# Matmul with batch normalisation: eight normalising instructions of VectorE rewritten to read their shift from PSUM

## The chip, the cores and the metric

The kernel runs on one core of a Trainium2 chip. A core has a matrix engine (TensorE, PE), a vector engine (VectorE, DVE), a scalar engine (ScalarE, ACT), a general engine (GpSimd, POOL), and a sync engine (SP) that here only issues DMAs. Operands lie in SBUF, results of TensorE in PSUM[...], and GpSimd is given no work on PSUM here. Each engine works its own queue in order, and engines wait for one another through semaphores. The metric is the device time of one execution in microseconds, shown as the median of several runs.

## The reference

The kernel computes a product and normalises each of its 768 columns over all 8192 rows:

```python
y = np.matmul(x, weight)                      # x (16, 512, 1024), weight (1024, 768)
mean = np.mean(y, axis=(0, 1), keepdims=True)
var = np.var(y, axis=(0, 1), keepdims=True)
y_norm = (y - mean) / np.sqrt(var + eps)
return (gamma * y_norm + beta).astype(np.float32)
```

No output value can be written before the statistics of its column are complete. For each column the kernel forms a scale and a shift, and an output is `y * scale + shift`.

## The kernel before

**Tiles.** The 768 columns are six tiles of 128 (`NT = 6`). The 8192 rows are 16 chunks of 512 (`CH = 512`, `C = 16`). The first three tiles (`GA = 3`) are treated as a group; the text calls tile `nt = 3` the fourth, `nt = 4` the fifth and `nt = 5` the sixth. A block is one tile of one chunk, 128 columns on the partitions by 512 rows, in bf16.

**First part.** While x arrives, TensorE computes the first three tiles for all chunks, and the others for the first five chunks (`EARLY = 5`). In twelve of the chunks the product of the three tiles lies with rows on the partitions (`mm_rows`), in four (`COLS`) with columns on the partitions (`mm`).

**Second part.** With the first three tiles complete, `affine_rows` forms their scale and shift, and `spread_rows` spreads both over all partitions by a product with ones: the scales into a PSUM tile `a_ps` of 128x384 (`aff[0]`), which stays there, the shifts into another, which ScalarE copies into SBUF (`sum1`). Then three streams of work run side by side:

- TensorE computes the remaining chunks of the fourth, the fifth and the sixth tile (`mm`, L196). Behind each block VectorE takes its statistics (`bn`, L316) and ScalarE copies it from PSUM to SBUF as bf16 (`keep`, L343).
- The twelve chunks with rows on the partitions are finished without TensorE: VectorE multiplies two row groups by the scales in PSUM (`norm_rows`, L283, 24 times, called a row product below), GpSimd adds the shifts from SBUF (`shift_rows`, L289, 24 times, called an add), SP stores.
- A tile with columns on the partitions and known statistics is finished in place: a block is normalised by ScalarE or VectorE (`norm`, L377 and L382), TensorE turns it back by transposes that stand between its other matmuls (`turn_y`, L398), ScalarE copies the turned block pair from PSUM into a piece of the SBUF ring (`out_copy`, L411), and SP stores it (L416).

**Scale and shift of the fourth and fifth tile.** `finish_var` has VectorE aggregate the statistics (L350), ScalarE take the square root (L351) and VectorE the reciprocal (L352). `finish_affine` then has ScalarE compute three columns of 128x1: `nscale` (L356), `scale` (L357) and `shift` (L358).

**Which engine normalises.** `outputs` goes through a tile in pairs of blocks, `b = 0` to `7`. While the row products run (the pair's due time `tb` lies below `tr + 2.0`, where `tr` is the due time of their end), the even block goes to ScalarE and the odd one to VectorE; later both go to VectorE. For the fourth tile this is so for `b = 0` to `6`, for the fifth only for `b = 0`.

**Order.** Every step is put into a list with a due time that is written by hand (`at`), the list is sorted, and the steps are issued in that order. `seq` ties each instruction to the one before it on its engine, so that the written order is the order of every queue. Semaphore waits between engines follow from the tiles that instructions read and write. PSUM tiles come from one pool of 8 buffers, one for each bank.

Of the kernel before, what the change touches and what calls it, by code (L numbers as in the profile page):

```python
# [10 lines left out]
def kernel(  # L11
# [23 lines left out]
    nc = tc.nc  # L35
# [3 lines left out]
    ALU = mybir.AluOpType  # L39
# [5 lines left out]
    P = 128  # L45
    NT = N // P
    KQ = K // 4
    CH = 512
# [9 lines left out]
    GA = 3  # L58
    COLS = (0, 5, 10, 15)
    NA = GA * P  # L60
# [16 lines left out]
    def seq(bi):  # L77

        ins = bi.ins
        prev = last.get(ins.engine)  # L80
        if prev is not None:
            tc.add_manual_dep(
                ins, prev,
                mybir.DependencyInfo(mybir.DependencyClass.NoSync, mybir.DependencyReason.DATA),
                reason="order",
            )
        last[ins.engine] = ins.name
        return bi
# [6 lines left out]
    scale = singles.tile([P, NT], f32)  # L95
    shift = singles.tile([P, NT], f32)
# [30 lines left out]
    xs, xT, py, ygrp, yrow, ops, ost, aff = {}, {}, {}, {}, {}, {}, {}, {}  # L127
# [140 lines left out]
    def spread_rows(i):  # L268

        a_ps = psum.tile([P, CH], f32, tag="b")  # L270
        aff[i] = a_ps[:, 0:NA]
        seq(nc.tensor.matmul(aff[i], full, aff["diag"][:, i], start=True, stop=True))  # L272
        if i == 1:
            seq(nc.scalar.copy(sum1, aff[i]))  # L274
# [24 lines left out]
    def y(nt, c):  # L299
        key, i = ((nt, c // GY), c % GY) if nt >= GA else ((0, c), nt)  # L300
        if key not in ygrp:
            y_sb = ypool.tile([P, GY, CH], bf16, tag="y")
            ygrp[key] = y_sb
        return ygrp[key][:, i]
# [49 lines left out]
    def finish_affine(nt):  # L354
        one = slice(nt, nt + 1)
        seq(nc.scalar.activation(nscale, rstd, AF.Identity, scale=ngamma[:, one]))  # L356
        seq(nc.scalar.activation(scale[:, one], rstd, AF.Identity, scale=gamma_sb[:, one]))  # L357
        seq(nc.scalar.activation(  # L358
            shift[:, one], mv[:, nt, 0:1], AF.Identity, bias=beta_sb[:, one], scale=nscale))

    def finish(nt):
        one = slice(nt, nt + 1)
        src = stats_of(nt) if nt < NT - 1 else fin
        seq(nc.vector.bn_aggr(mv[:, nt, :], src))
        seq(nc.scalar.activation(std[:, one], mv[:, nt, 1:2], AF.Sqrt, bias=eps_sb, scale=1.0))
        seq(nc.vector.scalar_tensor_tensor(
            tmp[:, one], mv[:, nt, 0:1], -1.0, gamma_sb[:, one], op0=ALU.mult, op1=ALU.mult,
        ))
        seq(nc.vector.reciprocal(rstd, std[:, one]))
        seq(nc.vector.tensor_mul(scale[:, one], rstd, gamma_sb[:, one]))  # L370
        seq(nc.vector.scalar_tensor_tensor(
            shift[:, one], tmp[:, one], rstd, beta_sb[:, one], op0=ALU.mult, op1=ALU.add,
        ))

    def norm(nt, c, eng):
        if eng == "act":
            seq(nc.scalar.activation(  # L377
                y(nt, c), y(nt, c), AF.Identity,
                bias=shift[:, nt:nt + 1], scale=scale[:, nt:nt + 1],
            ))  # L380
        else:
            seq((nc.vector if eng == "dve" else nc.gpsimd).tensor_scalar(  # L382
                y(nt, c), y(nt, c), scale[:, nt:nt + 1], shift[:, nt:nt + 1],
                op0=ALU.mult, op1=ALU.add,
            ))
# [39 lines left out]
    def at(t, fn, *args):  # L425
        events.append((t, len(events), fn, args))
# [85 lines left out]
    at(S + 0.9, affine_rows)  # L512
    at(S + 2.4, shift_diag)
    at(S + 4.4, spread_rows, 0)
    at(S + 5.6, spread_rows, 1)
    for nt in range(GA):
        at(S + 5.0, norm, nt, 0, "dve")
    ga = tuple(range(GA))
    tr, tk = S + 4.7, S + 6.3
    for c in range(C):  # L520
        if c in COLS:
            for nt in range(GA):
                if c:
                    at(tk - 3.4 + 0.8 * nt, norm, nt, c, "act")
            for s in range(0, RT, 2):
                at(tk + 0.7 * s, turn_y, ga, c * CH + s * P, 2)
                at(tk + 0.7 * s + 1.9, out_copy, ga, c * CH + s * P, "act")
                at(tk + 0.7 * s + 2.7, store, ga, c * CH + s * P, 2)
            tk += 9.6 if c else 7.2
        else:  # L530
            for s in range(0, RT, 2):
                at(tr, norm_rows, c, s)
                at(tr + 1.1, shift_rows, c, s)
                at(tr + 3.0, store_rows, c, s)
                tr += 1.85

    def outputs(nt, t0, step):
        for b in range(C // 2):
            tb = t0 + step * b
            if nt == NT - 2 and b >= C // 2 - HELD:  # L540
                held.append(b)
                continue
            for i in range(2):
                at(tb - 2.2 + 0.5 * i, norm, nt, 2 * b + i, "act" if tb < tr + 2.0 and i == 0 else "dve")
            at(tb, turn_y, (nt,), 2 * b * CH, 2 * RT)
            at(tb + 2.2, out_copy, (nt,), 2 * b * CH, "act")
            at(tb + 2.3, store, (nt,), 2 * b * CH, 2 * RT)
# [21 lines left out]
    for nt in range(GA, NT):  # L569
        for c in range(EARLY, C):  # L570
            if (nt, c) == (NT - 1, C - 1):
                for q in range(QPC):
                    at(pe, mm_half, q)
                    pe += 0.9
                    at(pe + 0.2, bn_half, q)
                    at(pe + (0.4 if q == 0 else 1.0), keep_half, q)
                at(pe - 2.4, sum_up)
                continue
            for jws in halves:
                unit(nt, c, MM_US / 2 + (0.12 if nt == GA else 0.17), jws)  # L580
        if nt < NT - 1:
            at(pe + 0.55, finish_var, nt)
            at(pe + 1.6, finish_affine, nt)
        else:
            at(pe + 0.55, finish, nt)
        if nt == GA:
            outputs(nt, S + 37.0, 2.3)
        elif nt < NT - 1:
            outputs(nt, pe + 4.6, 1.85)
        else:  # L590
            held_outputs(nt - 1, pe)
            last_outputs(nt, pe + 3.0)
# [39 lines left out]
```

## Time and profile before

| what | value |
|---|---|
| median of 8 runs | 219.83 us (219.18 to 220.51) |
| profiled execution | 220.45 us, of which its span is 218.6 us |
| TensorE matmul busy | 199.4 us, 91% of the span |
| VectorE busy | 155.7 us, 71% |
| GpSimd busy | 134.1 us, 61% |
| ScalarE busy | 121.2 us, 55% |
| chain that ended last | PE 74%, DVE 8%, DMA 6%, POOL 3% |
| VectorE normalising (L382) | 43 instructions, 22.0 us |
| GpSimd adds (L289) | 24 instructions, 44.2 us, from 134.8 to 182.5 us |
| VectorE row products (L283) | 24 instructions, from 133.3 to 180.4 us |

The span runs from the first instruction to the last; the rest of an execution's time lies around it. Busy time of an engine is no measure of what bounds the kernel: which engine the others wait for changes from stage to stage. The page's rows in slices of the span show the stages:

```profile
PE   7996999999999999999999999999999979997900
DVE  3220968887978789998744459988899999828900
ACT  2000563644453466645666414867767689986950
POOL 7786867778685589962558403999996973000000
```

Each digit is a slice of 5.5 us, in tenths of busy time. GpSimd's adds are the stretch of nines right of the middle. In the slice that starts at 175 us TensorE falls to 7, and in the last slices only transposes, copies and stores are left.

### The profile page before, as it was taken

The page shows a single profiled execution, that of the slowest core. Times are in us where ns is not written, and L with a number is a line of the kernel's source. Part 1 is how long each engine was busy: PE and PEld are TensorE (multiplying, and loading weights), DVE is VectorE, ACT ScalarE, POOL GpSimd, SP SyncE. Part 2 cuts the span into 40 slices and gives each one's busy share as a digit, 9 for nine tenths or more (in the row PEclk, how much of TensorE's full clock was granted, in tenths as well). Part 3 has the DMA queues.
Part 4 walks back from the last instruction along what each step waited for, and adds up shares of the span by engine and source line. Part 5 has one row for each costly group of instructions (what it writes and reads, how often), then busy time and mean ns, then how long its engine had stood idle before and what let it go on. Part 6 is the DMA issues. An engine that isn't in the chain of part 4 may idle for free.

```text
span 218.6 us, 3435 instructions
## 1 busy us (share of the span) xinstructions
PE 199.4 (91%) x1162; PEld 106.3 (49%) x1178; DVE 155.7 (71%) x263; ACT 121.2 (55%) x227; POOL 134.1 (61%) x153
## 2 busy tenths in 40 slices
PE   7996999999999999999999999999999979997900
PEld 2452454545554565645566544444444435554800
DVE  3220968887978789998744459988899999828900
ACT  2000563644453466645666414867767689986950
POOL 7786867778685589962558403999996973000000
PEclk9999999999999999999999999999999999999675
DMA  4999999999999999994000000798777989999998
GB/s 59 163 185 189 171 196 196 197 196 196 196 191 194 197 196 196 196 197 67 0 4 0 0 0 0 284 341 311 288 290 294 328 276 368 327 347 299 280 346 243
DMA packets 70161, 43.75 MB, mean 200 GB/s; under 512 B 4096, under 2 KB 69632, under 8 KB 70144
## 3 DMA queue, kind: packets, MB, share of 16 engines
q0 software_dynamic: 34624, 18.36, 61.6%
q1 hardware_dynamic: 35520, 25.18, 35.6%
q8 instruction: 9, 0.15, 0.3%
q14 instruction: 8, 0.07, 0.1%
HBM read 36.71 MB, written 25.17 MB: 283 GB/s over the span
## 4 chain that ended last, share of the span: by engine, by line
PE 74%; DVE 8%; DMA 6%; POOL 3%; issue 3%; ACT 2%; ACTq 1%; POOLq 0%
PE y_ps L196 38%; PE y_ps L186 29%; PE o_ps L398 6%; DMA w_sb<-in_weight_dram 3%; DMA ring<-in_x_dram 2%; DVE stats L316 2%; DVE y_sb L382 2%; DVE ring L283 2%; POOL w_sb L149 2%; DVE o_sb L283 1%; POOL ring L162 1%; PE y_ps L330 1%; ACT o_sb L411 1%; PE a_ps L272 1%; PE tot_ps L232 1%
## 5 line engine op out<-in xcount | busy, mean ns | idle before, releaser
L196 PE MATMUL y_ps<-xT_sb,w_sb 128*128 128x512 bf16 (+1 forms) x469 | 116.1, 381 | 3.6 <-DMA w_sb<-in_weight_dram 2.4
L196 PEld LDWEIGHTS <-w_sb 128*128 128x128 bf16 x484 | 45.9, 96 | 60.7 <-issue 4.6
L343 ACT CAST y_sb<-y_ps 128x512 bf16<-128x512 f32 x59 | 34.5, 585 | 55.0 <-DVE stats L316 52.1
L186 PE MATMUL y_ps<-w_sb,xT_sb 128*128 128x384 bf16 x384 | 63.4, 326 | 0.0
L316 DVE BATCH_NORM_STATS2 stats<-y_ps 128x6 f32<-128x512 f32 x58 | 39.2, 684 | 21.2 <-PE y_ps L196 20.0
L162 POOL DMA_DIRECT2D ring<-in_x_dram x72 | 45.2, 633 | 12.2 <-DVE xT_sb L174 6.2
L186 PEld LDWEIGHTS <-xT_sb 128*128 128x128 bf16 x384 | 37.5, 98 | 25.6
L212 POOL TENSOR_TENSOR sum<-sum,sq_sb 128x384 f32<-128x384 f32 x38 | 38.0, 1000 | 19.2 <-ACT sq_sb L208 18.0
L174 DVE STREAM_TRANSPOSE xT_sb<-ring 128x1024 f32<-128x1024 f32 (+1 forms) x34 | 39.5, 1167 | 12.1 <-DMA ring<-in_x_dram 12.1
L398 PE MATMUL o_ps<-ident,y_sb 128*128 128x128 bf16 x240 | 38.6, 231 | 4.0 <-DVE y_sb L382 2.5
L289 POOL TENSOR_TENSOR ring<-ring,sum 128x768 f32<-128x768 f32 x17 | 31.1, 1851 | 13.1 <-ACT sum L274 12.1
L215 DVE TENSOR_TENSOR sum<-y_ps,sum 128x384 f32<-128x384 f32 x48 | 26.1, 544 | 15.0 <-ACT sq_sb L208 14.1
L208 ACT ACTIVATE sq_sb<-y_ps 128x384 f32<-128x384 f32 x48 | 23.4, 492 | 15.6 <-PE y_ps L186 12.3
L221 ACT CAST y_sb<-y_ps 128x384 bf16<-128x384 f32 x48 | 22.8, 475 | 6.7 <-DVE sum L215 6.5
L411 ACT CAST ring<-o_ps 128x1024 f32<-128x1024 bf16 (+1 forms) x24 | 22.6, 951 | 4.1 <-PE o_ps L398 2.5
L398 PEld LDWEIGHTS <-y_sb 128*128 128x128 bf16 x240 | 21.0, 104 | 7.5 <-DVE y_sb L382 3.3
L382 DVE TENSOR_SCALAR y_sb<-y_sb,scale,shift 128x512 bf16<-128x512 bf16 x43 | 22.0, 563 | 0.0
L283 DVE TENSOR_TENSOR ring<-y_sb,a_ps 128x768 f32<-128x768 bf16 x17 | 15.8, 936 | 0.0
L289 POOL TENSOR_TENSOR o_sb<-o_sb,sum 128x768 f32<-128x768 f32 x7 | 13.1, 1876 | 2.9 <-DVE o_sb L283 2.9
L377 ACT ACTIVATE y_sb<-y_sb,shift,scale 128x512 bf16<-128x512 bf16 x17 | 13.5, 815 | 0.0
L155 PE MATMUL idle_ps<-idle_sb 128*128 128x512 bf16 x37 | 10.5, 449 | 1.2 <-DVE idle_sb L103 1.2
L411 ACT CAST o_sb<-o_ps 128x512 f32<-128x512 bf16 x16 | 7.9, 679 | 0.3 <-PE o_ps L398 0.3
(62 smaller groups left out, 50.1 us busy)
## 6 DMA issues: line engine op xcount, KB each, us to landing
ring<-in_x_dram POOLq DMA_DIRECT2D x56, 256.0 KB, 8.5
out_dram<-ring SPq DMA_DIRECT2D x25, 384.0 KB, 3.3
out_dram<-ring SPq DMA_DIRECT2D x16, 512.0 KB, 5.3
out_dram<-o_sb SPq DMA_DIRECT2D x16, 256.0 KB, 3.7
out_dram<-o_sb SPq DMA_DIRECT2D x7, 384.0 KB, 3.8
ring<-in_x_dram POOLq DMA_DIRECT2D x16, 128.0 KB, 5.4
w_sb<-in_weight_dram POOLq DMA_DIRECT2D x8, 96.0 KB, 4.9
w_sb<-in_weight_dram POOLq DMA_DIRECT2D x4, 192.0 KB, 6.4
```

The source lines that it names most:

```text
L162: seq(nc.gpsimd.dma_start(x_bf[32 * i:32 * i + 32], src[:, :, KQ * i:KQ * (i + 1)]))
L174: seq(nc.vector.transpose(dst[:, half, :, jw0:jw1], src[:, :, jw0:jw1]))
L186: seq(nc.tensor.matmul(y_ps, xT[c][:, jw, s * P:(s + 1) * P, e], w_sb[:, jw, e, 0:NA], start=(jw == 0 and e == 0), stop=(jw == JW - 1 and ...
L196: seq(nc.tensor.matmul(y_ps, w_sb[:, jw, e, nt * P:(nt + 1) * P], xT[c][:, jw, q0 * QR:q1 * QR, e], start=(jw == 0 and e == 0 and q0 == 0) ...
L212: seq(eng.tensor_add(acc, acc, py.pop(("sq", c, s))))
L215: seq(nc.vector.tensor_add(sum1, py["row", c, s][:, 0:NA], sum1))
L289: seq(nc.gpsimd.tensor_add(o_sb, o_sb, sum1[:, None, :].to_broadcast([P, 2, NA])))
L316: seq(nc.vector.bn_stats(stats_of(nt)[:, i, :], py[nt, c]))
L343: seq(nc.scalar.copy(y(nt, c), py.pop((nt, c))))
L382: seq((nc.vector if eng == "dve" else nc.gpsimd).tensor_scalar(y(nt, c), y(nt, c), scale[:, nt:nt + 1], shift[:, nt:nt + 1], op0=ALU.mult, ...
L398: seq(nc.tensor.transpose(dst, src, ident))
L411: seq(nc.scalar.copy(o_sb, src))
```

## The change

In `finish_affine`, for the fourth and the fifth tile, ScalarE also copies the new shift, one value for each partition, into a free column of the PSUM tile `a_ps` that holds the row scales: columns 384 and on, one for each tile. In `outputs`, a VectorE block that is normalised while the row products run gets a new form, `dve1`: a `scalar_tensor_tensor` that multiplies by the scale (a per-partition scalar in SBUF, as before) and adds a tensor, the shift's PSUM column read again for each of the 512 elements. Blocks of ScalarE, and VectorE blocks after the row products, stay as they were. These are blocks 1, 3, 5, 7, 9, 11 and 13 of the fourth tile and block 1 of the fifth, eight in all.

```diff
         a_ps = psum.tile([P, CH], f32, tag="b")
         aff[i] = a_ps[:, 0:NA]
+        if i == 0:
+            aff["shift"] = a_ps[:, NA:NA + NT - GA]
         seq(nc.tensor.matmul(aff[i], full, aff["diag"][:, i], start=True, stop=True))
...
         seq(nc.scalar.activation(
             shift[:, one], mv[:, nt, 0:1], AF.Identity, bias=beta_sb[:, one], scale=nscale))
+        if nt < NT - 1:
+            seq(nc.scalar.copy(aff["shift"][:, nt - GA:nt - GA + 1], shift[:, one]))
...
+        elif eng == "dve1":
+
+            seq(nc.vector.scalar_tensor_tensor(
+                y(nt, c), y(nt, c), scale[:, nt:nt + 1],
+                aff["shift"][:, nt - GA:nt - GA + 1].to_broadcast([P, CH]), op0=ALU.mult, op1=ALU.add,
+            ))
...
-                at(tb - 2.2 + 0.5 * i, norm, nt, 2 * b + i, "act" if tb < tr + 2.0 and i == 0 else "dve")
+                at(tb - 2.2 + 0.5 * i, norm, nt, 2 * b + i, "dve" if tb > tr + 2.0 else "dve1" if i else "act")
```

## The prediction

> **What bounds the kernel now.** I read the busy table by stage first. TensorE is over 98% busy from 20 to 150 us, so a change far from it is worth nothing there. One stage differs:
>
> ```profile
> 160.00:180.00 20.00, 17.89 (x116) 8.89 (x117) 19.64 (x25) 13.92 (x24) 16.52 (x10) 1.00 0.84 289
> 180.00:200.00 20.00, 19.81 (x153) 11.63 (x155) 14.61 (x32) 17.47 (x25) 1.99 (x1) 1.00 1.12 348
> ```
>
> The columns are the stretch, its length, busy time of PE, PE loads, VectorE, ScalarE and GpSimd, granted clock, DMA share and GB/s. In 160 to 180 us TensorE loses 2.1 us, at full clock, while VectorE is busy all the time. From 180 to 200 us it loses almost nothing. The waits of TensorE in 160 to 182 us name the cause:
>
> ```profile
> PE o_ps L398 <- ACT y_sb L377: 1.2, 2, 0.9
> PE o_ps L398 <- DVE y_sb L382: 0.8, 2, 0.5
> ```
>
> Transposes wait for normalised blocks. From the order of time, each stall counted as the late start beyond the usual 0.28 us step from the instruction before: 0.45 (starts 168.77), 0.65 (171.69), 0.40 (176.38) and 1.11 (179.75), **2.6 us** in sum. The last two name ScalarE, but ScalarE sat behind VectorE: its square root at 177.30 waited 0.98 us for the aggregate L350. Why VectorE is late, in order of time:
>
> ```profile
> 161.91 1.84 POOL L289 TENSOR_TENSOR o_sb<-o_sb,sum 128x768 f32<-128x768 f32 x1
> 163.70 1.85 POOL L289 TENSOR_TENSOR ring<-ring,sum 128x768 f32<-128x768 f32 x1
> 166.73 1.83 POOL L289 TENSOR_TENSOR o_sb<-o_sb,sum 128x768 f32<-128x768 f32 x1 [1.18 <-DVE o_sb L283]
> ```
>
> ```profile
> 162.32 3.38 DVE L382 TENSOR_SCALAR y_sb<-y_sb,scale,shift 128x512 bf16<-128x512 bf16 x1
> 167.09 1.62 DVE L382 TENSOR_SCALAR y_sb<-y_sb,scale,shift 128x512 bf16<-128x512 bf16 x1
> 173.02 0.45 DVE L382 TENSOR_SCALAR y_sb<-y_sb,scale,shift 128x512 bf16<-128x512 bf16 x1
> 177.71 1.24 DVE L382 TENSOR_SCALAR y_sb<-y_sb,scale,shift 128x512 bf16<-128x512 bf16 x1
> ...
> L382 DVE TENSOR_SCALAR y_sb<-y_sb,scale,shift x16: 404/405/411, 202.0 to 206.9; 128x512 bf16<-128x512 bf16 x16
> ```
>
> The same instruction takes 0.405 us once GpSimd is done (last line, min/median/max), but up to 3.38 us beside its adds: the first one ends at 165.70, just after the second of two adds (165.55). So the form waits for GpSimd. GpSimd then starves, since its next input stands behind that instruction on VectorE (1.18 us idle).
>
> **The change, part by part.**
>
> *Removed.* Eight such instructions: blocks 1, 3, ..., 13 of the fourth tile and block 1 of the fifth. From start to next start they cost 3.30 + 1.55 + 0.60 + 0.37 + 0.38 + 1.16 + 2.18 (the last two together) = 9.54 us.
>
> *Added on VectorE.* Eight scalar_tensor_tensor of 128x512, bf16 from SBUF with fp32 from PSUM. No such row exists. Bounds: 0.405 us (the free old form) and 0.936 us (L283, bf16 with PSUM at 768 elements). Statistics at 512 and 256 elements take 0.69 and 0.43, so 256 elements cost 0.26 us, and L283 scaled to 512 is 0.68; statistics of 512 PSUM elements take 0.69, in steps of 0.61. I take **0.61 per step, 4.9 us for eight**. Does it wait for GpSimd? L283, with the same kinds of operands, stays at 929 to 953 ns in all 24 cases, nearly all beside an add: no. [...] free form against new, eight cost 8 x (0.68 - 0.405) = 2.2 us more; by the rows, which contain the wait, VectorE saves 9.54 - 4.9 = 4.6 us. I go by the rows.
>
> *Added on ScalarE.* Two copies of 128x1. Nearest row: L356, 0.29 us; bounds 0.2 and 0.4. The first stands before the cast at 153.38, which had 0.58 us idle ahead of it: free. It waits for the row product at 151.79, done at 152.7, while the shift is done at 152.8. The next row product (153.27) now waits for the copy, done near 153.2: at most 0.1.
>
> *A new wait.* In the order of the changed program, the instruction for block 11 waits for ScalarE's **second** copy, the fifth tile's, though it reads another column. [...] By column the wait would go; by bank it stays, and decides the sum. Behind it on VectorE stand the statistics of the sixth tile's first block, the last row product (hence GpSimd's last add), and two more new instructions. The copy stands on ScalarE behind a cast, an output copy, a normalising (block 10) and three small steps.
>
> *Moved.* Nothing changes its place; no DMA is added, and SP and POOL stand in the same order. The PSUM bank of the row factors now lives until the last new instruction, where the next user is due later still: nothing.
>
> **The sum.** I carry the trace on from 162.32 us, with TensorE needing each block at its old time less what it has gained.
>
> - VectorE: block 1 162.93, row product 163.79, statistics (TensorE gives them near 164.2) 164.86, block 3 165.47 (before: about 168.6). TensorE wants it at 168.3: +0.45. Two row products and one statistics later block 5 at 168.4 (before 171.55): +0.65.
> - Statistics, row product 169.97, block 7 170.6, statistics (TensorE-bound) 171.4, row product 172.3, block 9 172.9, statistics 173.5, row product 174.35, aggregate 174.95, where before it ended at 177.26. ScalarE's normalising of block 8 ends near 173.7, wanted 174.9: +0.40.
> - ScalarE, held by the aggregate: square root 175.2, cast 175.7, output copy 176.6, block 10 at 177.3, wanted 177.15: +1.11 - 0.2. The three small steps need 0.19 + 0.19 + 0.38 (177.30 to 178.06), and the copy ends near 178.4.
> - Block 11 therefore runs 178.4 to 179.0, as late as before (178.95), though VectorE was ready at 175.45: 2.9 us idle. TensorE wants it at 180.89 - 2.4 = 178.5: -0.55.
> - Statistics 179.6, row product 180.5, two new instructions 181.7. Then the first old-form one waits for GpSimd's last add (180.5 to 182.3) and ends at 182.65; the old chain stood at 182.87. ScalarE's block 12 ends at 181.75, wanted 181.45: -0.3.
>
> Together 2.61 - 0.2 - 0.55 - 0.3 = **1.55 us**. What is late next: from 183 us VectorE and ScalarE are only 0.2 to 0.3 us ahead of before, and TensorE 1.55. That is covered by slack: VectorE idles 0.90, 1.14 and 1.55 us at 189 to 194, and the bank waits on output copies have about 2 us. If that cover were gone the gain would fall to 0.3. After TensorE's end a chain of small steps leads to the first late store (203.56). DMA lies nearly idle from about 201.4 to 203.4, and earlier stores come 3 us sooner in 165 to 180, so a shift of 1.55 fits. The final 16 stores then fill the queue at 346 GB/s as before.
>
> The profiled execution took 220.45 us (span 218.6, 1.85 outside). It gives 218.9. The median is 219.83, and the 3.38 us wait through two adds may be shorter in other runs, so I take 1.4 off it: **218.4 us**.
>
> **Rivals.**
>
> 1. *The wait for the second copy takes it all.* For: it idles a full engine for 2.9 us and its end is as late as before. Against: TensorE reaches block 11 with 1.1 us of its old stall taken away already. If the copy comes 1 us later than worked out, or the cover after 183 us is gone, 0.3 to 0.6 remains: 219.4, no change by the 0.3% (0.66 us) that can be told from noise.
> 2. *The new form is slow, and the wait passes it on: slower.* Five new instructions stand ahead of the aggregate, and the copy follows it by 3.4 us. Each 0.1 us on the form moves block 11 by 0.6 (five ahead and itself), less 0.7 us that VectorE waits for TensorE. Break-even is where block 11 ends at 180.9: 179.0 + 6x - 0.7 = 180.9, x = 0.43, a step of 1.04 us. At 1.2 us a step: 1.2 lost, about 221. Against: it would cost more than L283 with half as many elements again.
> 3. *The wait costs little, and the whole stall goes:* 2.4 us, 217.4, if ScalarE reaches its copy a microsecond earlier.
> 4. *The change doesn't do what it says:* the new form waits for GpSimd as the old. Then eight of up to 3 us remain: 219.9 or a little more. L283's even durations speak against it.
>
> **Numbers.** Forecast 0.58 (its own range 217.8 to 219.1); rival 1 0.20; rival 2 0.08; rival 3 0.09; rival 4 0.05. Faster by over 0.3%: the forecast, rival 3 and a little of rival 1, 0.68. Within: most of rival 1 and half of rival 4, 0.20. Slower: rival 2 and the rest, 0.12. Range 217.3 to 219.9: rival 3 at the low end, rival 1 at the high end, rival 2 left out.
>
> **What would show it.** L382's new line: eight at 0.65 to 0.72 us, none over 1. GpSimd's adds ending near 179 to 181, not 182.5. An idle of 2 to 3 us on VectorE before block 11, released by the new ScalarE copy. TensorE 1.3 to 1.8 us less stalled in 160 to 182, with a stall named after VectorE near 178.5. The forecast is wrong if new instructions exceed 1 us, if TensorE stalls after 183 us, or if DMA still works off old stores when the late ones start.

## The result and the profile after

| what | before | after |
|---|---|---|
| median | 220.08 us (218.58 to 222.19, 32 runs) | 217.56 us (216.66 to 218.60, 11 runs) |
| ratio after / before | | 0.9894 (0.9871 to 0.9916) |
| profiled execution (its span) | 220.45 (218.6) us | 217.78 (216.0) us |
| TensorE / VectorE busy | 199.4 / 155.7 us | 199.6 / 151.9 us |

The kernel is faster by about 2.3 us. The two profiled executions differ by 2.67 us, but part of that is not the change's: the first row product, before which both programs issue the same work, starts at 133.26 us before and at 132.27 us after. That 0.99 us is chance. All of it is there when the first matmul of `mm_rows` starts (25.75 us before, 24.76 after), and in each of the ten profiled runs below the first row product follows that matmul by 107.5 us. The page names one source of it, TensorE's first waits for the weights, 2.4 us before and 1.3 after. What follows is therefore measured from the first row product. The **stretch** from there to the first statistics of 256 rows (the last matmuls of the sixth tile) took 66.28 us before and 64.54 after, **1.74 us less**; to the end of the span it is 85.34 and 83.73, **1.61 us less**.

The busy table of the kernel after, in the same two stages and columns (stretch, its length, busy time of PE, PE loads, VectorE, ScalarE, GpSimd, granted clock, DMA share, GB/s):

```profile
160.00:180.00 20.00, 19.55 (x134) 10.13 (x135) 16.79 (x25) 16.56 (x28) 15.97 (x10) 1.00 0.99 342
180.00:200.00 20.00, 18.04 (x145) 10.81 (x146) 14.85 (x39) 16.26 (x24) 1.16 (x1) 1.00 1.01 309
```

From 160 to 180 us TensorE is now busy for 19.55 us instead of 17.89, while VectorE fell from 19.64 to 16.79. The second row isn't a new loss: the last stage, in which TensorE waits for normalised blocks in both kernels, now begins at 196.8 us and so lies inside it.

The waits of TensorE, and then those of VectorE, from 155 to 185 us (waited us, times, longest):

```profile
PE o_ps L408 <- DVE y_sb L387: 0.3, 1, 0.3
```

```profile
DVE y_sb L387 <- ACT a_ps L363: 2.8, 1, 2.8
```

Four named waits of 2.0 us have become one of 0.3. In their place VectorE waits once, for 2.8 us, for L363, ScalarE's new copy. The new instruction itself (min/median/max ns, first and last start):

```profile
L387 DVE SCALAR_TENSOR_TENSOR y_sb<-y_sb,scale,a_ps x8: 727/740/746, 161.3 to 179.7; 128x512 bf16<-128x512 bf16 x8
```

All eight take the same time, though GpSimd adds beside nearly all of them: the form doesn't wait for GpSimd. The old one took 0.41 to 3.38 us in this place. What became of the chain to block 11 is seen in the order of time, on ScalarE and then on VectorE (start, length, idle before in brackets):

```profile
173.70 0.29 ACT L353 ACTIVATE std<-mv,eps_sb 128x1 f32<-128x1 f32 x1 [0.92 <-DVE mv L352]
173.90 0.56 ACT L345 CAST y_sb<-y_ps 128x512 bf16<-128x512 f32 x1
174.36 1.01 ACT L421 CAST ring<-o_ps 128x1024 f32<-128x1024 bf16 x1
175.27 0.82 ACT L381 ACTIVATE y_sb<-y_sb,shift,scale 128x512 bf16<-128x512 bf16 x1
...
176.35 0.38 ACT L360 ACTIVATE shift<-mv,beta_sb,nscale 128x1 f32<-128x1 f32 x1
176.76 0.16 ACT L363 COPY a_ps<-shift 128x1 f32<-128x1 f32 x1
```

```profile
174.03 0.16 DVE L354 RECIPROCAL rstd<-std 128x1 f32<-128x1 f32 x1 [0.36 <-ACT std L353]
176.96 0.75 DVE L387 SCALAR_TENSOR_TENSOR y_sb<-y_sb,scale,a_ps 128x512 bf16<-128x512 bf16 x1 [2.77 <-ACT a_ps L363]
```

VectorE is ready at 174.19 us and needs only the fourth tile's shift, which has been in PSUM since 152 us. It waits for the fifth tile's copy, which stands on ScalarE behind a cast, an output copy, block 10 and three small steps. TensorE gets block 11 at 177.76 us, 0.47 us after it could have used it.

### The profile page after: what moved, and what is told of

Read it like the earlier page. It is cut to its first block, busy times and chain, and to the rows that moved or that the text cites. A ratio compares the mean times of both kernels' runs of the same rounds, so it can differ in the third digit from the quotient of the medians.

```text
span 216.0 us, 3439 instructions
## 1 busy us (share of the span) xinstructions
PE 199.6 (92%) x1162; PEld 106.5 (49%) x1178; DVE 151.9 (70%) x263; ACT 120.7 (56%) x229; POOL 133.8 (62%) x153
## 4 chain that ended last, share of the span: by engine, by line
PE 78%; ACT 5%; DMA 5%; DVE 3%; POOL 3%; issue 2%; ACTq 1%; POOLq 0%
PE y_ps L196 43%; PE y_ps L186 29%; PE o_ps L408 4%; ACT o_sb L421 3%; DMA w_sb<-in_weight_dram 3%; DMA ring<-in_x_dram 2%; POOL w_sb L149 2%; POOL ring L162 1%; ACT ring L421 1%; PE y_ps L332 1%; ACT y_sb L381 1%; DVE stats L318 1%; DVE y_sb L387 1%; PE a_ps L274 1%; PE tot_ps L232 1%
## 5 line engine op out<-in xcount | busy, mean ns | idle before, releaser
L345 ACT CAST y_sb<-y_ps 128x512 bf16<-128x512 f32 x59 | 35.1, 596 | 51.6 <-DVE stats L318 48.7
L392 DVE TENSOR_SCALAR y_sb<-y_sb,scale,shift 128x512 bf16<-128x512 bf16 x35 | 12.5, 415 | 0.0
L155 PE MATMUL idle_ps<-idle_sb 128*128 128x512 bf16 x37 | 11.0, 465 | 1.2 <-DVE idle_sb L103 1.2
```

What stands on the lines that cost most here:

```text
L345: seq(nc.scalar.copy(y(nt, c), py.pop((nt, c))))
```

## The experiments

**Theory A** is the account of the prediction: the gain is the old form's wait for GpSimd, and the wait for the second copy gives a part of it back. In each run it stands against a rival for that one step, which the expectation states. All kernels are edits of the kernel after. Runs 1 to 4 shared one set of runs of the kernel before (219.39 us, 13 runs), runs 5 to 8 another (219.64 us, 55 runs). Where nothing waits, TensorE's transposes follow one another by 0.28 us (0.06 us to the matmul between them and 0.23 us from it); a late start is what a transpose comes later than that. The last column sums the late starts from 160 us to the end of GpSimd's adds; a start that looks late only because matmul records are missing before it is left out.

| kernel | median us (runs) | ratio to before | stretch us | late starts us |
|---|---|---|---|---|
| before | | | 66.28 | 2.61 |
| after | 217.56 (11) | 0.9894 (0.9871 to 0.9916) | 64.54 | 0.73 |
| 1 after, again | 217.68 (9) | 0.9916 (0.9888 to 0.9945) | 64.53 | 0.73 |
| 2 own bank | 217.12 (6) | 0.9895 (0.9861 to 0.9929) | 63.74 | none |
| 3 fourth tile only | 216.85 (6) | 0.9877 (0.9840 to 0.9913) | 63.66 | none |
| 4 shift from SBUF | 221.68 (6) | 1.0107 (1.0071 to 1.0143) | 68.27 | 4.49 |
| 5 copies only | 219.71 (20) | 0.9999 (0.9979 to 1.0020) | 66.35 | 2.60 |
| 6 first two only | 219.62 (20) | 1.0002 (0.9978 to 1.0027) | 65.64 | 1.99 |
| 7 copy earlier | 218.32 (20) | 0.9947 (0.9923 to 0.9970) | 64.89 | 1.27 |
| 8 form doubled | 224.26 (4) | 1.0228 (1.0165 to 1.0290) | 71.35 | 4.89 |

From the statistics of 256 rows to the end of the span all ten profiled runs took 19.05 to 19.21 us: what the stretch gains arrives at the end. And up to run 7 the stretch is 63.6 to 63.8 us plus the late starts: they account for all of it.

### 1. The same kernel again

No edit.

> The changed kernel once more, to be compared with the others of this call. Both theories: 217.0 to 218.2 us. Theory A (the gain arises from 160 to 182 us alone, 1.6 to 1.7 us; the other 0.9 us of difference between the two profiles lie in the first 150 us, where the programs are the same, and are chance): the first row product starts anywhere from 132.0 to 133.6 us in this profile, and the stretch from it to TensorE's last product block is again 63.6 us within 0.3. Rival B (something in the first part became faster by 1 us): the first row product starts near 132.3 us again.

The profiled execution took 219.95 us, 2.17 more than the first, and its first row product started at 134.46 us, 2.19 later, which is outside the expected 132.0 to 133.6. In this run the page's row of the granted clock has an 8 in the two slices from 16.4 to 27.3 us, where the pages of all the others have a 9; how much of the 2.19 us that is was not tried. The stretch was 64.53, against 64.54. (Measured to the statistics of the last block of 512 rows, one block earlier, it is 63.65 and 63.66, near the 63.6 of the expectation.) So two executions of one program differ by over 2 us in the first part, and by 0.01 in the stretch: only the stretch, or the times of many runs, may be compared.

### 2. The second copy in its own bank

The fifth tile's shift goes to a free column of the other spread tile, which lies in another bank.

```diff
-        if i == 0:
-            aff["shift"] = a_ps[:, NA:NA + NT - GA]
+        aff["shift", i] = a_ps[:, NA:NA + 1]
...
-            seq(nc.scalar.copy(aff["shift"][:, nt - GA:nt - GA + 1], shift[:, one]))
+            seq(nc.scalar.copy(aff["shift", nt - GA], shift[:, one]))
...
-                aff["shift"][:, nt - GA:nt - GA + 1].to_broadcast([P, CH]), op0=ALU.mult, op1=ALU.add,
+                aff["shift", nt - GA].to_broadcast([P, CH]), op0=ALU.mult, op1=ALU.add,
```

> The fifth tile's shift goes into the other spread tile, that of the shifts, so into another PSUM bank; the rest is as changed. Theory A (block 11 waits for the second copy only because both columns share a bank): the 2.8 us idle of VectorE before block 11 is gone, GpSimd's last add ends about 3 us sooner, TensorE's 0.3 us stall for it goes: 0.3 to 0.5 us less than the changed kernel, about 217.2. Rival B (a second bank held for 45 us leaves TensorE short of PSUM): new waits of TensorE on y_ps or o_ps and 0.5 us or more slower than the changed kernel.

The groups by form (busy us, mean ns, idle before and what ended it), of the kernel after and of this one:

```profile
L387 DVE SCALAR_TENSOR_TENSOR y_sb<-y_sb,scale,a_ps 128x512 bf16<-128x512 bf16 x8 | 5.8, 738 | 2.8 <-ACT a_ps L363 2.8
```

```profile
L386 DVE SCALAR_TENSOR_TENSOR y_sb<-y_sb,scale,a_ps 128x512 bf16<-128x512 bf16 x8 | 5.8, 738 | 0.7 <-ACT a_ps L362 0.7
```

The idle time before block 11 is gone. The 0.7 us left is before the fifth tile's block, which does need its copy, and costs nothing. TensorE has no late start, and the stretch is 0.80 us shorter than after's: more than the 0.3 to 0.5 expected, since the late start of block 12 is gone too. So the wait was there because the two shifts share a PSUM tile, and not for data. In this program every PSUM tile has a bank to itself, so the run doesn't tell bank from tile. A shared tile alone makes no such wait, though: in the kernel before, block 11 read its column of the SBUF tile `shift` at 177.71 us, without waiting for ScalarE's write of the next column, which stands ahead of it in the written order:

```profile
179.96 0.38 ACT L358 ACTIVATE shift<-mv,beta_sb,nscale 128x1 f32<-128x1 f32 x1
```

In the time, 217.12 stands against 217.68 for the kernel after on the same chip; their intervals overlap, so the 0.8 us rests on the traces.

### 3. The fourth tile only

The fifth tile's block keeps the old form, and there is no second copy.

```diff
-        if nt < NT - 1:
+        if nt == GA:
             seq(nc.scalar.copy(aff["shift"][:, nt - GA:nt - GA + 1], shift[:, one]))
...
-                at(tb - 2.2 + 0.5 * i, norm, nt, 2 * b + i, "dve" if tb > tr + 2.0 else "dve1" if i else "act")
+                at(tb - 2.2 + 0.5 * i, norm, nt, 2 * b + i, "act" if tb < tr + 2.0 and i == 0 else "dve1" if tb < tr + 2.0 and nt == GA else "dve")
```

> The new form for the fourth tile's seven blocks alone: no second copy, and block 1 of the fifth tile has the old form again. Theory A: VectorE's idle before block 11 is gone as in the run with a bank of its own, and the old-form block of the fifth tile waits up to 1.8 us for GpSimd's last add at a time when TensorE does not yet need it: 0.2 to 0.5 us less than the changed kernel. Rival B (one old-form block is enough to bring a stall back): equal to the changed kernel or up to 1 us slower, with a TensorE stall named after L392 near 178 us.

The stretch is 63.66 us, like that of the second run, and the last add starts at 176.83 us. The fifth tile's block, in the old form again, took 1.69 us beside that add, and no transpose came late for it. So the eighth rewritten instruction brought nothing and brought the wait with it: two ways of taking the wait away give back 0.80 and 0.88 us.

### 4. The shift read from SBUF

The same instruction with the shift's column in SBUF as its second tensor. The two copies are left out (their lines are not shown).

```diff
-                aff["shift"][:, nt - GA:nt - GA + 1].to_broadcast([P, CH]), op0=ALU.mult, op1=ALU.add,
+                shift[:, nt:nt + 1].to_broadcast([P, CH]), op0=ALU.mult, op1=ALU.add,
```

> The new form, but it reads the shift column from SBUF, again for each element; no copies to PSUM. It tells what frees the instruction from GpSimd's adds. Theory A (the operand in PSUM does[...]): the eight instructions wait as the old form did, mean 1.2 us or more, and the time is that of the kernel before or up to 1.5 us above it, 219.8 to 221.5. Rival B (the slower form itself frees it, wherever the shift lies): all eight at 0.70 to 0.76 us, no wait for a copy, 217.0 to 217.4.

The groups by form, the instruction and the adds beside it; then the instruction's durations (min/median/max, ns) and GpSimd's last two adds in the order of time:

```profile
L383 DVE SCALAR_TENSOR_TENSOR y_sb<-y_sb,scale,shift 128x512 bf16<-128x512 bf16 x8 | 13.2, 1654 | 0.0
...
L289 POOL TENSOR_TENSOR o_sb<-o_sb,sum 128x768 f32<-128x768 f32 x7 | 14.0, 2003 | 3.8 <-DVE o_sb L283 3.8
```

```profile
L383 DVE SCALAR_TENSOR_TENSOR y_sb<-y_sb,scale,shift x8: 741/1340/3781, 161.6 to 182.6; 128x512 bf16<-128x512 bf16 x8
178.20 1.82 POOL L289 TENSOR_TENSOR ring<-ring,sum 128x768 f32<-128x768 f32 x1
182.20 2.18 POOL L289 TENSOR_TENSOR o_sb<-o_sb,sum 128x768 f32<-128x768 f32 x1 [2.18 <-DVE o_sb L283]
```

1654 ns on average instead of 738, and this kernel is slower than the one before by 1.07% (0.71 to 1.43). The form isn't slow in itself with its shift in SBUF: the one of the eight that began while no add ran, at 181.96 us, took the 741 ns of the PSUM form. The others lasted 0.86 to 3.78 us. The adds also lengthen: the same seven average 2003 ns here and 1876 before, and three adds in a row took 2.27 to 2.29 us. So the gain hangs on the operand in PSUM, not on the operation: beside the adds the old form took up to 3.38 us (the kernel before) and this one with its shift in SBUF up to 3.78, but the form with PSUM no more than 0.746. Whether GpSimd's adds wait as well or run slower can't be read from durations like these, which may contain a wait.

### 5. The copies alone

The two copies stay, and all blocks have the old form.

```diff
-                at(tb - 2.2 + 0.5 * i, norm, nt, 2 * b + i, "dve" if tb > tr + 2.0 else "dve1" if i else "act")
+                at(tb - 2.2 + 0.5 * i, norm, nt, 2 * b + i, "act" if tb < tr + 2.0 and i == 0 else "dve")
```

> Only the two ScalarE copies into PSUM are added to the kernel before; all VectorE blocks keep the old form and the SBUF shift, so nobody reads the copies. The stretch from the first row product to the sixth tile's last-but-one half statistics was 66.3 us before and 64.5 in both profiles of the changed kernel. Theory A (the copies are free, the form makes the difference): 66.1 to 66.5, no change of time. Rival B (the copies and the row product's wait for them cost): 66.7 or more.

Ratio 0.9999 (0.9979 to 1.0020), stretch 66.35 us against 66.28: the copies are free. The timeline of VectorE shows a wait of the same kind even here:

```profile
180.69 0.95 DVE L285 TENSOR_TENSOR o_sb<-y_sb,a_ps 128x768 f32<-128x768 bf16 x1 [1.00 <-ACT a_ps L363]
```

The last row product, which reads only the scales, waited 1.00 us for the copy of a shift. Nothing on TensorE came later for it: its late starts sum to 2.60 us, as before.

### 6. The first two blocks only

Blocks 1 and 3 have the new form, the other six the old one, and there is one copy.

```diff
-        if nt < NT - 1:
+        if nt == GA:
             seq(nc.scalar.copy(aff["shift"][:, nt - GA:nt - GA + 1], shift[:, one]))
...
-                at(tb - 2.2 + 0.5 * i, norm, nt, 2 * b + i, "dve" if tb > tr + 2.0 else "dve1" if i else "act")
+                at(tb - 2.2 + 0.5 * i, norm, nt, 2 * b + i, "act" if tb < tr + 2.0 and i == 0 else "dve1" if nt == GA and b < 2 else "dve")
```

> The new form for blocks 1 and 3 of the fourth tile alone, which waited 3.3 and 1.6 us; one copy. Theory A (as long as GpSimd has adds in store, an old-form instruction waits for the end of one or more, so a wait that is taken away at blocks 1 and 3 comes back at block 5 and later): L392 shows at least one wait over 1 us after them, TensorE is held at block 5 or behind, stretch 64.8 to 65.8. Rival B (the two long waits were the whole loss): 63.7 to 64.4.

VectorE in the order of time:

```profile
162.15 0.73 DVE L387 SCALAR_TENSOR_TENSOR y_sb<-y_sb,scale,a_ps 128x512 bf16<-128x512 bf16 x1
...
164.39 0.73 DVE L387 SCALAR_TENSOR_TENSOR y_sb<-y_sb,scale,a_ps 128x512 bf16<-128x512 bf16 x1
...
167.36 3.51 DVE L392 TENSOR_SCALAR y_sb<-y_sb,scale,shift 128x512 bf16<-128x512 bf16 x1
```

The wait through two adds has moved to the next old-form instruction, block 5, and is as long as it was at block 1 (3.38 us). Of the 1.74 us the stretch keeps 0.64, which the times can't show (1.0002, 0.9978 to 1.0027). The eight can't be judged one at a time.

### 7. The fifth tile's steps earlier

The three small steps and the copy of the fifth tile are due 1.0 us earlier, ahead of the cast, the output copy and block 10.

```diff
-            at(pe + 1.6, finish_affine, nt)
+            at(pe + (1.6 if nt == GA else 0.6), finish_affine, nt)
```

> The fifth tile's three small steps and its copy go right behind the square root on ScalarE, ahead of a cast, an output copy and block 10. Block 11 then waits 2 us less, but block 10 comes 1.1 us later on ScalarE. Theory A (TensorE needed block 10 within 0.1 us of when it came): the stall moves from block 11 to block 10 and grows from 0.5 to about 1.1 us, stretch 64.8 to 65.4. Rival B (block 11 alone was late): the stall goes, stretch 63.6 to 64.0 as with a bank of its own.

VectorE at block 11, and the waits of TensorE from 150 to 190 us:

```profile
175.49 0.75 DVE L387 SCALAR_TENSOR_TENSOR y_sb<-y_sb,scale,a_ps 128x512 bf16<-128x512 bf16 x1 [1.02 <-ACT a_ps L363]
```

```profile
PE o_ps L408 <- ACT y_sb L381: 1.1, 1, 1.1
```

VectorE's idle time fell from 2.77 to 1.02 us, and TensorE gained nothing (stretch 64.89 against 64.54): ScalarE now normalises block 10 at 176.78 us instead of 175.27, and TensorE waits there, 1.27 us late. A wait is not removed by a step that is moved ahead of another step which TensorE needs as soon.

### 8. The new form doubled

Ahead of each of the eight stands the same instruction, with its result written to a scratch area that nothing reads.

```diff
         elif eng == "dve1":
+            seq(nc.vector.scalar_tensor_tensor(
+                sum2[:, 0:CH // 2].bitcast(bf16), y(nt, c), scale[:, nt:nt + 1],
+                aff["shift"][:, nt - GA:nt - GA + 1].to_broadcast([P, CH]), op0=ALU.mult, op1=ALU.add,
+            ))
             seq(nc.vector.scalar_tensor_tensor(
```

> Each of the eight new instructions runs twice, the first time into scratch: VectorE's price of a block doubles and nothing else changes. It tests how the sum carries such a price: five ahead of the aggregate and the block itself, so six times, less the 0.3 us that VectorE waits for TensorE between. At 0.7 to 0.8 us each: block 11 later by 3.9 to 4.5 us, stretch 68.0 to 69.0, so 2 to 3 us slower than the kernel before. Rival B (VectorE has slack there, the gain came from GpSimd being free of the waits): under 66.3, still not slower than before.

The direction is right and the size is not: the stretch is 71.35 us, over 2 us beyond the expectation, and the kernel is 2.3% slower than the one before, about 5 us instead of 2 to 3. From start to start a block pays 0.77 us more, and by the prediction's arithmetic (6x - 0.7) block 11 should come 3.9 us later than after; its transposes start at 182.18 instead of 177.76, 4.4 later. That part is nearly right. TensorE's late starts are 1.46 (175.34 us), 2.17 (179.78) and 1.26 (182.18), together 4.16 more than after. The stretch grew by 6.81; the rest, 2.65, is in the clock column of the busy table (the last row shows a part of the first again):

```profile
173.00:181.00 8.00, 4.68 (x31) 2.14 (x29) 4.83 (x9) 5.85 (x12) 3.62 (x2) 1.00 0.56 184
181.00:184.00 3.00, 1.90 (x9) 0.98 (x9) 2.96 (x5) 1.54 (x3) 0.25 (x1) 0.55 0.89 320
184.00:187.00 3.00, 3.00 (x16) 1.59 (x15) 2.93 (x6) 0.97 (x2) 1.57 (x1) 0.50 0.67 208
187.00:190.00 3.00, 3.00 (x25) 1.78 (x23) 3.00 (x9) 2.57 (x4) 0.00 (x0) 0.82 0.32 114
...
177.87:181.28 3.41, 1.30 (x8) 0.57 (x8) 0.69 (x1) 3.38 (x8) 0.82 (x1) 1.00 0.50 157
```

The granted clock fell to 0.50 at 181.28 us, after 3.41 us in which TensorE was busy for 1.30, and came back at 188.11. TensorE's timeline shows what that means for a step:

```profile
182.18 0.29 PE L411 MATMUL o_ps<-ident,y_sb 128*128 128x128 bf16 x1 [1.10 <-DVE y_sb L390]
...
182.79 0.63 PE L196 MATMUL y_ps<-xT_sb,w_sb 128*128 128x512 bf16 x1
183.33 0.63 PE L196 MATMUL y_ps<-xT_sb,w_sb 128*128 128x512 bf16 x1
```

It is 0.54 us from one of these matmuls to the next, instead of 0.28, from 182.2 to about 188 us. Six microseconds in steps of 0.54 do what takes 3.1 in steps of 0.28, so they cost about 2.9. The longest late start was 2.2 us, and the 3.41 us before the fall were not idle: TensorE was busy in them for 1.30 us. The last section sets other falls of the clock beside this one.

## Why the prediction was right

- **TensorE loses 2.6 us to the old form's wait for GpSimd: shown.** With the new form and no wait for the second copy (runs 2 and 3) the stretch loses 2.54 and 2.62 us, the whole of it. With two SBUF inputs (run 4) the stall is there and larger, 4.49 us of late starts against 2.61.
- **0.61 us a step: a little low.** Measured are 0.73 to 0.75 us in duration (0.68 estimated) and 0.65 to 0.67 from start to next start, where the next instruction was ready. Reckoned against the old form's free time of 0.405 us, eight of the new one cost 2.2 us more by the prediction's estimate. That doesn't decide, since of the eight old-form instructions in this stage only one took its free time (0.41 us), and their mean is 1.27.
- **The copies are free: shown** (run 5). Each takes 0.163 us, below the lower bound of 0.2.
- **Block 11 waits for the second copy, though it reads another column: shown** (run 2; that it is by bank and not by PSUM tile is not). The prediction had 2.9 us of idle VectorE and 0.55 lost; measured 2.77 and 0.47. On the clock of the kernel before (0.99 us added) block 11 began at 177.95 us instead of the predicted 178.4, because two terms were a little smaller than worked out: the aggregate ended 0.3 us earlier (173.66, or 174.65 on that clock, against 174.95), and on ScalarE the copy took 0.16 us and not 0.3.
- **The small terms: in part.** Block 12 lost 0.26 (0.3 predicted). Block 10's 0.2 did not occur, because ScalarE was ahead of the working by that time. So the late starts fell by 2.61 - 0.73 = 1.88 us, a little more than the 1.3 to 1.8 named as a sign.
- **The stall at 176.38 us: right, by another wait than the one named.** The square root at 177.30 comes too late to hold block 8. On ScalarE block 8 stood behind a cast that had waited for VectorE's statistics:

```profile
174.11 0.58 ACT L343 CAST y_sb<-y_ps 128x512 bf16<-128x512 f32 x1 [0.54 <-DVE stats L316]
```

- **The sum: 1.55 us predicted (its terms give 1.56), 1.74 measured in the stretch and 1.61 to the end of the span.** The slack after 183 us and the DMA queue let nearly all of it through. In the times the gain is larger in one set (0.9894) than the sum's 0.993, and in the other (0.9916) consistent with it. Both are drawn from programs whose first part varies by 2 us, so a few tenths stay open. Of the numbers on record, 217.56 lies nearer to rival 3's 217.4 than to the forecast's 218.4. It is the trace that tells the two apart: block 11 does wait, and the stretch gains 1.74 us and not the 2.4 of rival 3. Scaling the gain down to 1.4 for the median has no support: the late starts of the old form sum to 2.61 us before and to 2.60 in run 5.
- **One sign was wrong.** GpSimd's adds were to end near 179 to 181 us. They end at 181.16, which on the clock of the kernel before is 182.15, hardly earlier than 182.5. The sum's own working had 182.3: the last row product stands behind block 11. As a sign it told nothing.
- **The rivals.** The whole gain (rival 3) is what runs 2 and 3 reach. Rival 2's arithmetic held for block 11 (3.9 us by it, 4.4 measured in run 8), but its price was too low: it lacked the clock. Its own formula gives a loss of 0.9 us at a step of 1.2, and not the 1.2 that it states.

Runs 2 and 3 have the shortest stretches of all, with 217.12 and 216.85 us, which their intervals don't tell apart. Run 3 is the simpler one: it is the change without the second copy and the fifth tile's block.

## What to carry to other kernels

Where a VectorE instruction's durations scatter while GpSimd works on SBUF, as here from 0.41 to 3.38 us, suspect waiting: look for the same operation in a stage where GpSimd is done, and for one with a PSUM operand beside it, and price the change by those two rows. Rewriting a few of them may only move the wait, as in run 6; leaving one that nothing waits for cost nothing, as in run 3. Before a value is parked in the free columns of a PSUM tile, ask who writes that tile later: here block 11 waited 2.77 us for that writer, and in run 5 the last row product 1.00 us, though both read other columns.

## What the runs showed of the hardware that was not expected

- TensorE's granted clock went from 1.00 to 0.50 for 6.8 us after 3.41 us in which TensorE was busy for 1.30, with no late start above 2.2 us (run 8). In the last stage it fell to 0.50 twice in the kernel before, at 203.55 and 210.38 us, and twice in the kernel after, at 201.18 and 208.00 us; in the 3.41 us ahead of these falls TensorE was busy for 1.75, 1.22, 1.75 and 0.97 us. In run 4, with late starts of up to 1.51 us, the clock stayed at 1.00 from 160 to 186 us, where TensorE was busy for 9.02 of the first ten us, 8.11 of the next ten and 5.00 of the last six. The busy times are those of the profile, in which a few matmul records are missing; how much of a pause brings a fall was not tried.
- A `scalar_tensor_tensor` of 128x512 took 0.74 us with its second tensor in PSUM and 1.65 us on average with it in SBUF, beside the same adds, though that tensor is one column read again and again; the one that began while no add ran took 0.74 us from SBUF too (run 4).
- A copy of 128x1 by ScalarE into PSUM took 0.163 us, about half of an activation of the same size (0.28 to 0.38).
- Kernels with the same first part reached their first row product between 131.41 and 134.46 us in the ten profiled runs, and the same kernel at 132.27 and at 134.46.
